# Row sums of 64 MB: the first buffer's two loads, cut by partitions in place of rows

## Chip, cores and metric

The kernel runs on one core of a Trainium2 chip. The metric is the device time of one execution in microseconds (us); the figure given is the median of three executions. The profile is that of one further execution, taken by the hardware profiler.

## What is computed

The input x is a float32 array of 32 x 512 x 1024. The output is the sum over the last axis, one float32 number for each of the 16,384 rows of 1024:

```python
def reference(x: np.ndarray) -> np.ndarray:
    return np.sum(x, axis=-1).astype(np.float32)
```

So 67.11 MB are read from HBM and 65 KB are written. There is one addition for each number read.

## The kernel before

The 16,384 rows are handled in two blocks (BLOCKS = (112, 16)). In a block, each of the 128 partitions owns a run of neighbouring rows: 112 of them in the first block, 16 in the second. Since the rows of a partition lie one behind the other in HBM, a load of 16 rows is, for each partition, one contiguous run of 64 KB in HBM, and goes to 64 KB of that partition in SBUF. Neighbouring partitions start 448 KB apart in HBM.

The first block is read in seven loads of 16 rows (G = 16), 8.39 MB each, into a pool of three buffers called xt. After each load the reduction helper rows_dve (L47) lets VectorE (DVE) sum 16 rows of all partitions in one instruction, from 128x16384 to 128x16 numbers. For the seventh load VectorE sums nine rows and ScalarE (ACT) seven, one activation with an accumulator each (L55). ScalarE then issues the store of the first block's results (L99), as 104 and 24 partitions.

The second block is the end of the kernel. Its 16 rows are loaded in five pieces: 9, 4 and 2 rows into an xt buffer (L105), and the last row in two pieces of 544 and 480 numbers into a tile of its own, tail (L108). VectorE and ScalarE share these pieces, and the store (L128) follows.

What sets the order: all loads are issued by the SP engine, in program order, on one DMA queue (q1 in the profile). The first three buffers are free at the start, so the first four DMAs are issued without a wait; each later load waits on SP until VectorE is done with the buffer that it will fill. The stores of the first block go through ScalarE's queue (q10). A block of code at the end of the file moves SP's first two loads (EARLY = 2) ahead of the start barrier into the entry block of the program.

The first buffer is special. It is filled by two DMAs instead of one, both issued at L89, as the cut points at L87 say:

```python
parts = (0, 1, m) if done + c == 0 else (0, m)
```

That is, for the very first buffer, one row of all 128 partitions (128 runs of 4 KB, 0.5 MB) and then fifteen rows of all 128 partitions (128 runs of 60 KB, 7.5 MB). The reduction of this buffer is one instruction over all sixteen rows, so it waits for both.

Of the kernel before, what the change touches and what calls it, by code (L numbers as in the profile page):

```python
# [1 line left out]

# [4 lines left out]

F32 = mybir.dt.float32
ADD = mybir.AluOpType.add
COPY = mybir.ActivationFunctionType.Copy  # L10
X = mybir.AxisListType.X

BLOCKS = (112, 16)
G = 16
ACT_ROWS = 7
CUT = 544
EARLY = 2


@with_exitstack  # L20
def row_sums(
    ctx: ExitStack,
    tc: tile.TileContext,
    x: bass.AP,
    out: bass.AP,
):
    nc = tc.nc
    P = nc.NUM_PARTITIONS

    x_flat = x.flatten_outer_dims()  # L30
    R, D = x_flat.shape
    C = R // P
    assert R % P == 0 and sum(BLOCKS) == C
    out_flat = out.rearrange("a (b c) -> (a b c)", c=1)

    xpool = ctx.enter_context(tc.tile_pool(name="x", bufs=3))
    rpool = ctx.enter_context(tc.tile_pool(name="res", bufs=1))


    tail = rpool.tile([P, D + 16], F32, name="tail")  # L40
    part = tail[:, CUT + 14 : CUT + 15]
    nc.vector.memset(tail[:, CUT + 15 : CUT + 16], 0.0)  # L42
    seen = rpool.tile([P, 2], F32, name="seen")
    pairs = [rpool.tile([P, D // 2], F32, name=f"pairs{i}") for i in range(3)]

    def rows_dve(xt, res, j, n, c):
        nc.vector.tensor_reduce(  # L47
            out=res[:, c : c + n],
            in_=xt[:, j * D : (j + n) * D].rearrange("p (j d) -> p j d", d=D),
            axis=X,  # L50
            op=ADD,
        )

    def sum_act(v, acc):
        return nc.scalar.activation(out=v, in_=v, func=COPY, accum_out=acc)  # L55

    by_act = []

    def rows_act(xt, res, j, n, c):
        for i in range(n):  # L60
            by_act.append(
                sum_act(xt[:, (j + i) * D : (j + i + 1) * D], res[:, c + i : c + i + 1])
            )

    def pairs_dve(v, a, b, acc, pairs):
        h = (a + b) // 2
        nc.vector.tensor_tensor_reduce(  # L67
            out=pairs[:, 0 : h - a], in0=v[:, a:h], in1=v[:, h:b], scale=1.0, scalar=0.0,
            op0=ADD, op1=ADD, accum_out=acc,
        )  # L70

    def block(r0, n):
        x_b = x_flat[r0 : r0 + P * n].rearrange("(p c) d -> p (c d)", p=P)
        out_b = out_flat[r0 : r0 + P * n].rearrange("(p c) -> p c", p=P)
        return x_b, out_b, rpool.tile([P, n], F32, name=f"res{r0}")

    full = C - G
    done = 0
    for b, n in enumerate(BLOCKS):
        x_b, out_b, res = block(done * P, n)  # L80
        final = b == len(BLOCKS) - 1
        whole = n - G if final else n
        c = 0
        while c < whole:
            m = min(G, whole - c)
            xt = xpool.tile([P, G * D], F32, tag="xt", name="xt")
            parts = (0, 1, m) if done + c == 0 else (0, m)  # L87
            for i, k in zip(parts, parts[1:]):
                nc.sync.dma_start(  # L89
                    out=xt[:, i * D : k * D], in_=x_b[:, (c + i) * D : (c + k) * D]  # L90
                )
            a = ACT_ROWS if done + c + m == full else 0
            rows_dve(xt, res, 0, m - a, c)
            rows_act(xt, res, m - a, a, c + m - a)
            c += m
        if not final:

            for i, k in ((0, 104), (104, P)):
                nc.scalar.dma_start(out=out_b[i:k], in_=res[i:k])  # L99
        done += n  # L100

    xt = xpool.tile([P, G * D], F32, tag="xt", name="xt")
    cuts = [0, 9, 13, 15]
    for i, k in zip(cuts, cuts[1:]):
        nc.sync.dma_start(out=xt[:, i * D : k * D], in_=x_b[:, (c + i) * D : (c + k) * D])  # L105
    last = 15 * D
    for i, k, gap in ((0, CUT, 0), (CUT, D, 16)):
        nc.sync.dma_start(  # L108
            out=tail[:, i + gap : k + gap],
            in_=x_b[:, c * D + last + i : c * D + last + k],  # L110
        )

    by_act.clear()
    for i, k in zip(cuts[:2], cuts[1:3]):
        h = (k - i) // 2
        rows_dve(xt, res, i, h, c + i)
        rows_act(xt, res, i + h, k - i - h, c + i + h)
    pairs_dve(xt, 13 * D, 14 * D, res[:, c + 13 : c + 14], pairs[2])
    rows_act(xt, res, 14, 1, c + 14)
    pairs_dve(tail, 0, CUT, part, pairs[0])  # L120


    nc.vector.tensor_copy(out=seen, in_=tail[:, CUT + 14 : CUT + 16])  # L123
    pairs_dve(tail, CUT + 14, D + 16, res[:, c + 15 : c + 16], pairs[1])


    tc.keep_in_program_order(nc.sync.keepalive_nop([nc.sync.lower_ap(res[:, c + 14 : c + 15])]))
    store = nc.sync.dma_start(out=out_b, in_=res)  # L128
    for i in by_act:
        tc.declare_no_dep(store.ins, i.ins, reason="the wait is in the nop before it")  # L130


def kernel(tc: tile.TileContext, x: bass.AP, out: bass.AP):
    row_sums(tc, x, out)
    tc.close()
    tc.compile()  # L136

    sp = mybir.EngineType.SP  # L140
    fn = tc.nc.m.functions[0]
    entry, body = None, None
    for blk in fn.blocks:
        ops = [i for i in blk.instructions if i.engine == sp]
        if entry is None:
            entry = blk
        elif any(i.opcode == "DMACopy" for i in ops):
            body = blk
            break
    code = list(body.instructions)  # L150
    loads = [i for i in code if i.engine == sp][:EARLY]
    for load in loads:
        assert load.opcode == "DMACopy" and not load.sync_info.on_wait
        code.remove(load)
    body.instructions = code
    code = list(entry.instructions)
    at = next(k for k, i in enumerate(code) if i.engine == sp and i.opcode == "Drain")
    code[at:at] = loads
    entry.instructions = code

# [1 line left out]
_INS = ['x']  # L162
_OUTS = [((32, 512), 'float32')]


# [23 lines left out]
```

## Time and profile before

| what | value |
|---|---|
| median of 3 executions | 162.14 us (162.09 to 162.2) |
| the profiled execution: its own time | 162.21 us |
| the profiled execution: span from first to last instruction | 160.4 us |
| DVE busy | 121.4 us (76%) |
| ACT busy | 17.2 us (11%) |
| HBM read | 67.11 MB, 419 GB/s over the span |
| a reduction of 128x16384 on DVE | 17.22 us |

How to read it: the page gives busy times by engine, the span in 40 slices with the share of the DMA engines and the rate in GB/s in each, the DMA queues with their packets, the chain of work that ended last, and groups of instructions with their mean duration and the idle time ahead of them. A name such as xt<-in_x_dram means that the tile xt is written from the input in HBM. A packet of a queue is one piece of data that one DMA engine moved, or one write of four bytes to a semaphore by which an engine reports that its share of a load is done. There are 16 DMA engines.

### The profile page before, as it was taken

Reading aid. Unit: us, or ns where it says so; the run is one execution under the profiler, and the core shown is the slowest. Engines: PE = TensorE matmul, PEld = TensorE weight load, DVE = VectorE, ACT = ScalarE, POOL = GpSimd, SP = SyncE. Lnnn points to the kernel's source line nnn. Section 1 sums busy time; section 2 is a strip of 40 time slices with the busy share of each in tenths; the row PEclk is TensorE's granted clock in tenths of the full one; section 3 lists DMA queues with packets and bytes.
Section 4 is the critical chain, followed back from the end, with each engine's and each line's share of the span. In section 5 each row is a group of like instructions: output and inputs, shape, how many; then the busy total and the mean of one; then the engine's idle time right before and its main releaser. Section 6 shows DMA issues by size and latency. Waiting matters only on the chain.

```text
span 160.4 us, 122 instructions
## 1 busy us (share of the span) xinstructions
DVE 121.4 (76%) x17; ACT 17.2 (11%) x31; POOL 0.2 (0%) x4
## 2 busy tenths in 40 slices
DVE  0000059997799959999499994999949998698883
ACT  0000000000000000000000000000000000695892
POOL 0000000000000000000000000000000000000000
DMA  9988996996996996996996996997998999998992
GB/s 376 490 368 368 490 523 261 523 523 261 523 523 261 523 523 261 523 523 261 523 507 278 523 490 294 523 474 310 523 425 359 523 392 392 441 395 369 431 393 79
DMA packets 2169, 67.18 MB, mean 419 GB/s; under 512 B 505, under 2 KB 633, under 8 KB 889
## 3 DMA queue, kind: packets, MB, share of 16 engines
q1 hardware_dynamic: 2016, 67.12, 97.4%
q10 hardware_dynamic: 153, 0.06, 0.1%
HBM read 67.11 MB, written 0.07 MB: 419 GB/s over the span
## 4 chain that ended last, share of the span: by engine, by line
DMA 75%; DVE 22%; SPq 0%; issue 0%; DVEq 0%
DMA xt<-in_x_dram 75%; DVE res L47 21%; DVE pairs L67 1%; SPq L105 0%; DVE seen L123 0%; DVE tail L67 0%; DVEq L136 0%; DVE res L67 0%
## 5 line engine op out<-in xcount | busy, mean ns | idle before, releaser
L47 DVE TENSOR_REDUCE res<-xt 128x16 f32<-128x16384 f32 (+3 forms) x9 | 119.8, 13308 | 35.1 <-DMA xt<-in_x_dram 35.1
L55 ACT ACT_TABLE_LOAD x1 | 1.3, 1283 | 137.9 <-DMA xt<-in_x_dram 137.9
L55 ACT ACTIVATE xt<-xt 128x1024 f32<-128x1024 f32 x15 | 15.6, 1043 | 2.5 <-DMA xt<-in_x_dram 2.5
L55 ACT ACTIVATION_READ_ACCUMULATOR xt<-xt 128x1 f32 x15 | 2.8, 186 | 0.0
L42 DVE MEMSET tail<- 128x1 f32 x1 | 0.1, 59 | 1.3 <-PEq L173 1.3
L67 DVE CUSTOM_DVE_ANT_0 pairs<-xt 128x512 f32<-128x512 f32 x1 | 0.7, 692 | 0.3 <-DMA xt<-in_x_dram 0.3
L67 DVE CUSTOM_DVE_ANT_0 pairs<-tail 128x272 f32<-128x272 f32 (+1 forms) x2 | 0.9, 426 | 0.0
L123 DVE COPY seen<-tail 128x2 f32<-128x2 f32 x1 | 0.2, 168 | 0.0
L67 DVE DVE_READ_ACCUMULATOR2_ANT res<- 128x1 f32 x2 | 0.2, 82 | 0.0
L173 POOL MEMSET const-bfloat16-1.0<- 128x1 bf16 x1 | 0.1, 103 | 0.0
L173 POOL MEMSET const-uint8-127<- 128x1 uint8 x1 | 0.1, 102 | 0.0
L173 POOL MEMSET const-float32-1.0<- 128x1 f32 x1 | 0.1, 100 | 0.0
L173 POOL MEMSET const-float32-0.0<- 128x1 f32 x1 | 0.1, 99 | 0.2 <-issue 0.2
L67 DVE DVE_READ_ACCUMULATOR2_ANT tail<- 128x1 f32 x1 | 0.1, 80 | 0.0
## 6 DMA issues: line engine op xcount, KB each, us to landing
xt<-in_x_dram SPq DMA_DIRECT2D x1, 7680.0 KB
xt<-in_x_dram SPq DMA_DIRECT2D x1, 4608.0 KB, 32.6
xt<-in_x_dram SPq DMA_DIRECT2D x1, 2048.0 KB, 37.1
xt<-in_x_dram SPq DMA_DIRECT2D x1, 1024.0 KB, 39.2
xt<-in_x_dram SPq DMA_DIRECT2D x1, 512.0 KB, 3.6
tail<-in_x_dram SPq DMA_DIRECT2D x1, 272.0 KB, 39.3
tail<-in_x_dram SPq DMA_DIRECT2D x1, 240.0 KB, 39.2
xt<-in_x_dram SPq DMA_DIRECT2D x6, 40.8
```

The costliest lines, as they stand in the source:

```text
L42: nc.vector.memset(tail[:, CUT + 15 : CUT + 16], 0.0)
L47: nc.vector.tensor_reduce(out=res[:, c : c + n], in_=xt[:, j * D : (j + n) * D].rearrange("p (j d) -> p j d", d=D), axis=X, op=ADD,)
L55: return nc.scalar.activation(out=v, in_=v, func=COPY, accum_out=acc)
L67: nc.vector.tensor_tensor_reduce(out=pairs[:, 0 : h - a], in0=v[:, a:h], in1=v[:, h:b], scale=1.0, scalar=0.0, op0=ADD, op1=ADD, accum_out ...
L123: nc.vector.tensor_copy(out=seen, in_=tail[:, CUT + 14 : CUT + 16])
L173: nc = _bacc.Bacc("TRN2", target_bir_lowering=False, num_devices=1)
```

## The change

The first buffer is still filled by two DMAs, issued in the same place and order. They are now cut by partitions: first all 16 rows of partitions 0 to 15 (16 runs of 64 KB, 1 MB), then all 16 rows of partitions 16 to 127 (112 runs of 64 KB, 7 MB). The other loads name the same data as before, though they are written in the new form.

```diff
@@ -84,11 +84,10 @@
         while c < whole:
             m = min(G, whole - c)
             xt = xpool.tile([P, G * D], F32, tag="xt", name="xt")
-            parts = (0, 1, m) if done + c == 0 else (0, m)
+
+            parts = (0, 16, P) if done + c == 0 else (0, P)
             for i, k in zip(parts, parts[1:]):
-                nc.sync.dma_start(
-                    out=xt[:, i * D : k * D], in_=x_b[:, (c + i) * D : (c + k) * D]
-                )
+                nc.sync.dma_start(out=xt[i:k, 0 : m * D], in_=x_b[i:k, c * D : (c + m) * D])
             a = ACT_ROWS if done + c + m == full else 0
             rows_dve(xt, res, 0, m - a, c)
             rows_act(xt, res, m - a, a, c + m - a)
```

The lists of instructions of both kernels are the same on every engine but for line numbers (these two loads are issued at L90 instead of L89, and every later line has a number one lower) and the shapes of SP's first two loads: 128x1024 and 128x15360 before, 16x16384 and 112x16384 after.

## The prediction

> **What bounds the kernel now.** I read the slices of the page first, then the timeline of VectorE, then the chain, then stretches cut at the starts of the reductions.
>
> ```profile
> DVE  0000059997799959999499994999949998698883
> ...
> DMA  9988996996996996996996996997998999998992
> GB/s 376 490 368 368 490 523 261 523 523 261 523 523 261 523 523 261 523 523 261 523 507 278 523 490 294 523 474 310 523 425 359 523 392 392 441 395 369 431 393 79
> ```
>
> The DMA row has no gap from the first slice to the last but one. The rates jump between 261 and 523 only because a long packet is booked in one slice; over three slices they are level. VectorE has holes at regular distances. The timeline shows what it waits for there:
>
> ```profile
> 21.84 17.22 DVE L47 TENSOR_REDUCE res<-xt 128x16 f32<-128x16384 f32 x1 [20.46 <-DMA xt<-in_x_dram]
> 41.13 17.22 DVE L47 TENSOR_REDUCE res<-xt 128x16 f32<-128x16384 f32 x1 [2.06 <-DMA xt<-in_x_dram]
> 60.48 17.22 DVE L47 TENSOR_REDUCE res<-xt 128x16 f32<-128x16384 f32 x1 [2.13 <-DMA xt<-in_x_dram]
> 79.82 17.22 DVE L47 TENSOR_REDUCE res<-xt 128x16 f32<-128x16384 f32 x1 [2.12 <-DMA xt<-in_x_dram]
> ```
>
> Columns: start, duration, instruction, idle time ahead and its releaser. A buffer of 8.39 MB arrives every 19.35 us (60.48 - 41.13), its reduction takes 17.22, and the rest is waiting for data. 8.39 MB in 19.35 us are 434 GB/s, 27.1 for each of 16 DMA engines. Each engine carries 8 of the 128 runs of 64 KB, so a run takes 19.35 / 8 = 2.42 us on its engine.
>
> ```profile
> 58.38 40.78 DMA xt<-in_x_dram
> ...
> 117.29 39.21 DMA xt<-in_x_dram
> 156.50 0.02 issue
> 156.52 0.69 DVE pairs L67
> ```
>
> The chain ends with a load and then 1.6 us of short sums. Its reductions (17.23 us pieces) are there because they release the buffers, but a release comes well ahead of need: buffer 1 is free at 21.84 + 17.22 = 39.06, when load 2 has 2 us to go and load 3 is queued whole, some 21 us of DMA work. So the DMA stream never runs dry, and **whatever delays the slowest DMA engine's stream by d at its start delays the end by d**. Nothing later has slack to absorb it.
>
> ```profile
> 0.00:4.00 4.00, 0.06 (x1) 0.00 (x0) 0.20 (x4) 1.00 1.02 377
> 4.00:21.84 17.84, 0.00 (x0) 0.00 (x0) 0.00 (x0) 1.00 1.03 445
> 41.13:60.48 19.35, 17.22 (x1) 0.00 (x0) 0.00 (x0) 1.00 1.00 434
> ```
>
> Columns: stretch and length; DVE, ACT, POOL busy; PE clock; DMA share; GB/s. Even the stretch that holds the change runs near the later rate, so there is little to gain there and much to lose.
>
> [...]
>
> [...]
>
> ```profile
> q1 hardware_dynamic: 2016, 67.12, 97.4%
> q10 hardware_dynamic: 153, 0.06, 0.1%
> ```
>
> ScalarE's queue q10 carries only the stores of 104 and 24 partitions: 128 runs of data and 25 reports, which is 13 (104 / 8) and 12 (24 / 2). Likewise q1: 13 loads of 128 + 16 packets and a store of 144 are 2016. So I expect the new loads on 16 engines each, with 1 and with 7 runs for an engine.
>
> [...]
>
> [...]
>
> [...]
>
> **The change part by part.** The sum starts from the profiled execution: 160.4 us of span and 1.81 outside it make 162.21, 0.07 over the median of 162.14. As the change is a difference within the span, I add it to the median.
>
> *Issue.* Two DMAs before, two after, same place, no wait added. SP's time for them (0.85 us for both in the timeline) stays: 0. Their descriptors are fewer (16 rows, not 128, in the first); the DMA view of the first microseconds has its first bytes at about 1.0 us. I take 0 and keep a small gain for a rival.
>
> *First load, removed.* 0.52 MB in 128 runs, landed 3.6 us after issue; its share of the stream at 434 GB/s is 1.2 us. *First load, added.* 1.05 MB, one run for each engine. [...] Each engine then comes to its next run 9.67 - 2.42 = **7.25 us late**. [...] I take 7.25.
>
> *Second load, added.* 112 runs, 7 for an engine, 16.9 us if no two engines meet. [...] How the runs are dealt out I don't know. I take blocks of seven neighbours: [...] 7 / 4 x 2.42 = **4.2 us**. From below: 0 (later loads fill the holes). From above: [...] 4 x 2.42 = 9.7 us.
>
> *Everything behind.* Six loads of 128 runs[...]: no loss and no recovery, since the engines already run at their full rate. VectorE starts each reduction later by the same amount; it keeps its 2.1 us of idle time for each load, which hides nothing needed. SP's waits for free buffers move along: 21 us of queued work cover them as long as the engines differ by less than that. ScalarE and the end are unchanged: 0.
>
> Sum: 7.25 + 4.2 = 11.45 us. 162.14 + 11.45 = **173.6 us**; from the bounds, 169.4 (7.25 + 0) to 179.1 (7.25 + 9.7).
>
> **The rivals.**
>
> *No change, 162.1.* The DMA engine is the limit[...]. Each engine has 1 + 7 = 8 runs before load 2, as much as before. The same follows if the change doesn't reach the engines as I think: if a partition belonged to an engine whatever the load[...]. For it: 434 GB/s is 16 times one engine's rate[...]. Against it: [...] for the second form the 13 and 12 reports.
>
> *Faster, 161.6.* One mechanism: the cold start. In the view of the first 4 us the first load's data runs from about 1.0 to 3.3 us, 2.3 us for 1.2 us of bytes. So 1.1 us at most are to be won; if it is the short reads that each pay for a cold start, and one long run for each engine pays once, I put the gain at half of that, 0.55 us. [...]
>
> *Much slower, about 213.* If the second load deals neighbouring partitions to different engines in turn, [...] 7 x 7.25 = 51 us. Against it: the engines needn't stay in step[...].
>
> **How the numbers follow.** [...] much slower 5%, no change 11%, faster 12%. A measurement of this kernel can tell about 0.2% (0.3 us) from no change. So faster 0.12, same 0.11, slower 0.77. The likeliest case's own range is 169.4 to 179.1. As it holds only 72%, the range must reach down over the no-change and most of the faster case: 161.5 to 179.1; left out are the much slower case and the tails.
>
> **What would show it.** Right: the first reduction starts near 33 us instead of 21.84, the later ones again 19.35 apart; the rate in the first 10 us falls to about a quarter of 434 GB/s; q1 counts 2016 - 128 = 1888 packets[...]. If the first reduction starts 7 us late and no more, the second load's term is wrong; if it starts over 17 us late, the dealing is. Wrong altogether: the first microseconds at 434 GB/s with 16 partitions being filled, and the first reduction still near 21.8.

## The result and the profile after

| | before | after |
|---|---|---|
| median of 4 executions | 162.12 us (162.04 to 162.2) | 184.4 us (183.82 to 184.55) |
| profiled execution, span | 160.4 us | 182.6 us |
| DVE busy / ACT busy | 121.4 / 17.2 us | 121.4 / 17.2 us |
| first reduction starts | 21.84 us | 44.39 us |

The changed kernel takes 1.137 times as long (95% interval 1.134 to 1.139), 22.3 us more. The forecast was 173.6, in a range of 161.5 to 179.1: the direction was right, the size (11.45 us) was half of what came, and the range was missed.

These are lines of the page of the changed kernel: the 40 slices (each now 182.6 / 40 = 4.6 us long), and the two DMA queues with their packets, megabytes and share.

```profile
DVE  0000000002999599978999599959995999689784
...
DMA  9199799888999988999999988999999989999990
GB/s 230 29 201 230 230 402 215 201 215 330 445 459 459 431 388 373 445 445 459 445 459 459 431 388 373 431 459 445 459 459 459 431 359 402 450 396 421 423 364 14
...
q1 hardware_dynamic: 1888, 67.12, 97.0%
q10 hardware_dynamic: 153, 0.06, 0.1%
```

The DMA row still shows engines that are busy nearly all the time: 97.0% of their time, as before (97.4%). But a busy engine is not one that moves bytes. Of the first nine slices eight show 230 GB/s or less and one 402 (a long packet is booked whole in the slice in which it starts); from the eleventh on the rate is back at its old level. This is how the shortage looks here: a full busy row at half the rate. The 1888 packets are the 2016 of before less 128, so both loads ran on all 16 engines (1 and 7 runs for each), as foretold.

VectorE's timeline in the changed kernel (start, duration, instruction, idle time and its releaser):

```profile
44.39 17.22 DVE L47 TENSOR_REDUCE res<-xt 128x16 f32<-128x16384 f32 x1 [43.01 <-DMA xt<-in_x_dram]
63.67 17.22 DVE L47 TENSOR_REDUCE res<-xt 128x16 f32<-128x16384 f32 x1 [2.06 <-DMA xt<-in_x_dram]
83.02 17.22 DVE L47 TENSOR_REDUCE res<-xt 128x16 f32<-128x16384 f32 x1 [2.13 <-DMA xt<-in_x_dram]
102.36 17.22 DVE L47 TENSOR_REDUCE res<-xt 128x16 f32<-128x16384 f32 x1 [2.12 <-DMA xt<-in_x_dram]
```

All the lost time lies ahead of the first line: 44.39 - 21.84 = 22.55 us. After it the buffers arrive 19.3 us apart, as before, with the same 2.1 us of idle time. Nothing is given back. The short sums at the end of the chain start at 178.71 in place of 156.52, 22.2 us later:

```profile
178.71 0.69 DVE pairs L67
```

Three stretches of the changed kernel: about the first load, most of the second, and the time from the first reduction to the second one (the last column is GB/s):

```profile
1.00:9.00 8.00, 0.06 (x1) 0.00 (x0) 0.00 (x0) 1.00 1.17 147
9.00:39.00 30.00, 0.00 (x0) 0.00 (x0) 0.00 (x0) 1.00 1.03 240
44.39:63.67 19.28, 17.22 (x2) 0.00 (x0) 0.00 (x0) 1.00 0.98 425
```

The kernel before, in the stretch from 9 to 39 us:

```profile
9.00:39.00 30.00, 17.16 (x1) 0.00 (x0) 0.00 (x0) 1.00 1.02 443
```

There are two slow stretches, and the second is the long one. The trace also has each packet. Put in order of their starts and taken 16 at a time (one run of 64 KB for each engine), the packets of the first buffer show how long each run took. Times are in us from the first packet:

```
changed kernel     starts        shortest  median  longest
run 0 (16-load)     0.0 -  0.7     7.64     8.54     9.25
run 1 (112-load)    7.7 -  9.8     5.12     5.47     6.40
run 2              13.7 - 15.0     4.75     4.75     4.90
run 3              18.5 - 19.8     2.98     3.25     4.81
run 4              21.9 - 24.6     3.81     3.89     4.47
run 5              25.8 - 28.4     4.21     4.54     4.84
run 6              30.0 - 33.1     4.71     4.72     4.89
run 7              34.7 - 37.8     4.51     4.53     4.87
```

A line of this table, that is, the 16 runs that the engines carry at the same turn, is called a row of the load below. In a load of 128 partitions such a run takes 2.42 us. Here every run of every engine is slow. In five of the seven rows of the second load even the shortest of 16 runs takes 1.7 to 2.1 times as long. That is not what the prediction had, where the seven rows were to lose 7 / 4 of 2.42 us, 4.2 us in all.

### The profile page after: what moved, and what is told of

Read it like the earlier page. It is cut to its first block, busy times and chain, and to the rows that moved or that the text cites. A ratio compares the mean times of both kernels' runs of the same rounds, so it can differ in the third digit from the quotient of the medians.

```text
span 182.6 us, 122 instructions
## 1 busy us (share of the span) xinstructions
DVE 121.4 (66%) x17; ACT 17.2 (9%) x31; POOL 0.2 (0%) x4
## 3 DMA queue, kind: packets, MB, share of 16 engines
q1 hardware_dynamic: 1888, 67.12, 97.0%
## 4 chain that ended last, share of the span: by engine, by line
DMA 68%; DVE 29%; another core or an unknown queue 1%; SPq 1%; issue 0%; DVEq 0%
DMA xt<-in_x_dram 68%; DVE res L47 28%; DVE pairs L67 1%; SPq L104 0%; SPq L90 0%; DVE seen L122 0%; DVEq L47 0%; DVE tail L67 0%; DVE res L67 0%; DVEq L135 0%
```

## The experiments

All times are medians (of two executions for probe4, probe19 and pstep6, of 22 for nocut, of four for the others), and "over before" is the distance from the median of the kernel before in the same group of runs (162.05 us for the first four, 162.12 for probe11 to probe0 without nocut, 161.97 for nocut, probe4, probe19 and pstep6).

| kernel | us | over before | ratio, 95% interval |
|---|---|---|---|
| eight16 | 216.15 | 54.1 | 1.334 (1.328 to 1.339) |
| step7 | 183.98 | 21.9 | 1.134 (1.131 to 1.138) |
| step8 | 183.44 | 21.4 | 1.131 (1.128 to 1.134) |
| src8 | 217.39 | 55.3 | 1.340 (1.336 to 1.345) |
| probe11 | 167.9 | 5.8 | 1.036 (1.034 to 1.037) |
| probe18 | 174.25 | 12.1 | 1.074 (1.073 to 1.076) |
| probe16 | 172.23 | 10.1 | 1.062 (1.060 to 1.064) |
| probe0 | 181.14 | 19.0 | 1.117 (1.115 to 1.119) |
| nocut | 162.2 | 0.2 | 1.0013 (1.0007 to 1.0020) |
| probe4 | 173.75 | 11.8 | 1.072 (1.070 to 1.075) |
| probe19 | 173.24 | 11.3 | 1.069 (1.067 to 1.071) |
| pstep6 | 172.53 | 10.6 | 1.065 (1.062 to 1.068) |

### How is the second load dealt, and on which side is the limit?

The first four kernels change only how the first buffer is filled. They are built from the changed kernel; the edits of eight16 and src8 are shown against it, those of step7 and step8 against eight16.

*eight16: eight loads of 16 neighbours.*

```diff
-            parts = (0, 16, P) if done + c == 0 else (0, P)
+            cuts = tuple(slice(g, g + 16) for g in range(0, P, 16)) if done + c == 0 else (slice(0, P),)
-            for i, k in zip(parts, parts[1:]):
+            for s in cuts:
-                nc.sync.dma_start(out=xt[i:k, 0 : m * D], in_=x_b[i:k, c * D : (c + m) * D])
+                nc.sync.dma_start(out=xt[s, 0 : m * D], in_=x_b[s, c * D : (c + m) * D])
```

> The first buffer is filled by eight loads of 16 neighbouring partitions each (0-15, 16-31, and so on)[...]. Theory A (the load of 112 partitions deals single partitions to the engines in turn[...]): the runs of each engine are the same as in the changed kernel, so 184 us, within 1.5. Theory B (the 112 partitions are dealt in blocks of seven neighbours[...]): another sequence, [...] eight times 9.67 us in place of 19.35 gives up to 162 + 58 = 220 us, less if an engine's next run overlaps the one before. Theory C ([...] something in HBM or in the count of runs is): unlike both, about 162 plus eight times the 7 us of the first load, 218 us.

Measured 216.15, 54.1 over before. The changed kernel's 184.4 is far off, so theory A (partitions dealt out one at a time) falls. The runs after the first take 9.29 to 9.34 us each. Theories B and C both allow this number; step8 and src8 tell them apart.

*step7: the dealing in blocks of seven, written out as seven loads.*

```diff
-            cuts = tuple(slice(g, g + 16) for g in range(0, P, 16)) if done + c == 0 else (slice(0, P),)
+            cuts = (slice(0, 16),) + tuple(slice(16 + j, P, 7) for j in range(7)) if done + c == 0 else (slice(0, P),)
```

> The load of partitions 0-15 is kept; the other 112 partitions are loaded by seven loads of 16 partitions, each stepping by seven (16, 23, 30, ...)[...]: the dealing in blocks of seven, written out. Theory A: not the order of the changed kernel; [...] the 7.25 us of the first load and 2.4 to 9.7 for the rest: 172 to 179 us. Theory B: the same runs as in the changed kernel, 184 us within 1.5.

Measured 183.98, within 0.5 us of the changed kernel. Its first reduction:

```profile
43.99 17.22 DVE L47 TENSOR_REDUCE res<-xt 128x16 f32<-128x16384 f32 x1 [42.20 <-DMA xt<-in_x_dram]
```

Its runs have the same pattern, row for row: medians 8.56, 5.26, 4.66, 3.11, 4.05, 4.55, 4.65, 4.43 us. So the load of 112 partitions deals blocks of seven neighbours, as the prediction took it (theory B). The dealing was right; the price of it was not.

*step8: eight loads of 16 partitions, eight apart.*

```diff
-            cuts = tuple(slice(g, g + 16) for g in range(0, P, 16)) if done + c == 0 else (slice(0, P),)
+            cuts = tuple(slice(g, P, 8) for g in range(8)) if done + c == 0 else (slice(0, P),)
```

> Eight loads of 16 partitions that step by eight (g, g+8, ..., g+120). [...] Same bytes, same length of run, same 16 engines as eight loads of neighbours. [...] (theories A and B): every run takes twice its 2.42 us, 8 x 4.84 - 19.35 = 19.3 us more than before: 181 us, and no run shorter than 4.7 us in the middle of it. Theory C [...]: the distance between partitions in SBUF makes no difference to it; the same time as eight loads of neighbours.

Measured 183.44, 21.4 over before where theories A and B gave 19.3. Against eight16, with the same bytes, run length, engines and count of loads, a different distance between partitions in SBUF and HBM takes off 33 us. At the median a run takes 5.10 us in six of the seven loads after the first (4.89 in the other), so 16 of them at a time move 16 x 65.5 KB / 5.10 us = 206 GB/s. One stretch in the middle of its filling:

```profile
9.00:39.00 30.00, 0.00 (x0) 0.00 (x0) 0.00 (x0) 1.00 1.02 210
```

210 GB/s are about half of the 434 at which the loads of 128 partitions arrive.

*src8: neighbours in SBUF, eight apart in HBM.*

```diff
-            parts = (0, 16, P) if done + c == 0 else (0, P)
-            for i, k in zip(parts, parts[1:]):
-                nc.sync.dma_start(out=xt[i:k, 0 : m * D], in_=x_b[i:k, c * D : (c + m) * D])
+            if done + c == 0:
+                for g in range(8):
+                    nc.sync.dma_start(
+                        out=xt[16 * g : 16 * g + 16, 0 : m * D],
+                        in_=x_b[g:P:8, c * D : (c + m) * D],
+                    )
+            else:
+                nc.sync.dma_start(out=xt[:, 0 : m * D], in_=x_b[:, c * D : (c + m) * D])
```

> As the eight loads of 16 neighbouring partitions, but each reads its 16 runs of HBM eight partitions apart (the rows of the first 2048 x 7 of the input land in other partitions, so part of the sums stand in another order). [...] (A and B): the same time as the eight loads of neighbours, within 1 us. Theory C with HBM as the cause: the time of the eight loads that step by eight, whose HBM addresses these are.

Measured 217.39, with runs of 9.39 us. That is 1.24 us more than eight16, a little outside the 1 us that was expected at most, and 34 us more than step8. The HBM addresses are those of step8, the time is within 0.6% that of eight16. The limit is on the SBUF side. Theory C falls: its HBM form here, and the form with the count of runs by step8, which has the same count as eight16.

### Is a whole row slow, or a few of its runs?

In the changed kernel each row starts behind another slow one. To look at one set of partitions alone, the kernel before got two additional loads of it, ahead of all else, into the two buffers that are filled later. They fetch data that the later loads overwrite; the sums are those of the kernel before.

```diff
         c = 0
+        if b == 0:
+            for _ in range(2):
+                probe = xpool.tile([P, G * D], F32, tag="xt", name="xt")
+                nc.sync.dma_start(out=probe[11:117:7, :], in_=x_b[11:117:7, 0 : G * D])
         while c < whole:
```

The four kernels of this group have the slices 11:117:7 (probe11, shown above), 18:124:7 (probe18), 16:122:7 (probe16) and 0:16 (probe0). By the dealing that step7 writes out, 16:122:7 is run 1 of the table above and 18:124:7 is run 3; 0:16 is run 0.

> The kernel before, preceded by two additional loads of 16 partitions, 64 KB each, into the two buffers that are not filled first: partitions 11, 18, ..., 116[...]. The cost of the probe is the time over the kernel before. [...] each run takes 2.42 us as in a load of 128 partitions, and the two cost 4.8 us: 167 us. If a load of 16 partitions is slow for another reason (few partitions, runs far apart, one run for each engine), they cost what two loads of partitions 0-15 cost, some 18 us.

Measured 5.8 us for two loads, where 4.8 were expected. The second load's runs take 2.42 to 2.63 us (those of the first 3.23 at the median). So a load of 16 partitions, one run for each engine, far apart, can be as fast as any other: with these partitions it is.

> The same with partitions 18, 25, ..., 123[...]. Theory D[...]: the median run takes well over 2.42 us[...]. Theory E[...]: the median run takes 2.42 us and two of 16 runs 4.8 us; the time is still up to 9.7 us longer, since the two slowed engines set the end.

> The same with partitions 16, 23, ..., 121[...]. Theory D: the median run takes 4.65 us as in the changed kernel, and the two loads cost 9.3 us: 171.4 us. Theory E: four of 16 runs take 4.8 us, the median 2.42 us; the time again up to 9.7 us longer.

> The same with partitions 0 to 15[...]. [...] 9.33 us a run, as in the eight loads of neighbours, 18.7 us for the two: 180.8 us. [...]

The 16 runs of the second probe load, in us:

```
           partitions          fastest 14 runs    slowest 2 runs
probe11    11, 18, ..., 116     2.42 to 2.43       2.43, 2.63
probe18    18, 25, ..., 123     2.42 to 2.48       6.95, 6.99
probe16    16, 23, ..., 121     4.98 to 5.05       5.05, 5.05
probe0     0, 1, ..., 15        9.58 to 9.64       9.64, 9.64
```

The stretch from 6 to 11 us, in which the second probe load gives way to the first real one, in probe11 (the last column is GB/s):

```profile
6.00:11.00 5.00, 0.00 (x0) 0.00 (x0) 0.00 (x0) 1.00 1.15 486
```

The same stretch in probe18:

```profile
6.00:11.00 5.00, 0.00 (x0) 0.00 (x0) 0.00 (x0) 1.00 1.03 290
```

And in probe16:

```profile
6.00:11.00 5.00, 0.00 (x0) 0.00 (x0) 0.00 (x0) 1.00 0.59 123
```

A packet is booked whole where it starts, so 486 and 123 are not rates of the moment; only the order of the three counts, and the table of runs is the better evidence. For the partitions of probe18 theory E holds: 14 runs go at 2.42 to 2.48 us and two are slow. For those of probe16 theory D holds: all 16 take 4.98 to 5.05 us. Neither theory holds for both. The trace doesn't name the engine of a packet, so which partitions the two long runs of probe18 fill is not shown. The size of probe18 was missed: 12.1 us, not up to 9.7. Its two long runs took 6.97 us in the second load, more than twice 2.42. (These runs start at 4.74 and 4.76 us, just as the two slowest runs of the first load end, which fits two engines that are late both times.) By then the other engines were already at the first real load (the 290 GB/s above). Whether that is what makes these two runs so long was not tried.

probe0 prices the first load of the changed kernel by itself: 19.0 / 2 = 9.5 us for each load, 9.5 - 2.42 = 7.1 us more than a load whose runs take 2.42 us.

One thing these probes don't separate: a set of other partitions in SBUF is also a set of other addresses in HBM, and no probe reads the HBM addresses of one set into the partitions of another, as src8 did for the loads of neighbours.

### Two long runs or sixteen: three more sets

The same probe, with the slices 4:110:7, 19:125:7 (run 4 of the table above) and 4:95:6; and one kernel without any cut (nocut, built from the changed kernel).

> The probe of two additional loads, with partitions 4, 11, ..., 109[...]. Theory F[...]: 14 runs of the second load take 2.42 us, two take 4.8 us or more, as with partitions 18 to 123. Theory G[...]: all 16 runs take some 5.0 us, as with partitions 16 to 121.

Measured: 13 of the runs of the second load at 2.42 to 2.59 us, one at 2.65, two at 5.99 and 6.39. As in probe18 only two runs are slow, so theory G falls.

> The probe with partitions 19, 26, ..., 124[...]. Theory F: 14 runs of the second load at 2.42 us, two at 4.8 us or more. [...] if all 16 runs are slow here too, the free engines with partitions 18 to 123 were an exception.

Measured: 13 runs at 2.42 us, one at 2.68, two at 6.32 and 6.49. A third set in which only two runs are slow.

> The probe with partitions 4, 10, ..., 94 (steps of six)[...]. Theory F: all 16 runs of the second load at about 5.0 us, as with partitions 16 to 121[...]. Theory H[...]: part of the runs stay at 2.42 us. [...]

Measured: all 16 runs at 4.96 to 5.11 us, as in probe16. No run stayed at 2.42 us, so theory H falls for this set. The numbers of theory F came in all three sets: of the five sets with long runs in steps of six or seven, three have two long runs and two have sixteen. Why a set belongs to the one kind or the other is not shown; what the author sorted them by beforehand was an assumption. The rows of the 112-load go the same way: run 1, with the partitions of probe16, has a median of 5.47 us, and runs 3 and 4, with those of probe18 and probe19, have 3.25 and 3.89 us (not 2.42. In these rows engines that are late from the row before are still at work, which may be why; this is argued, not tried). Runs 2, 5, 6 and 7 have medians of 4.53 to 4.75 us; their partitions were not tried alone.

*nocut: the first buffer by one load.*

```diff
-EARLY = 2
+EARLY = 1
-            parts = (0, 16, P) if done + c == 0 else (0, P)
+            cuts = (slice(0, P),) if done + c == 0 else (slice(0, P),)
-            for i, k in zip(parts, parts[1:]):
+            for s in cuts:
-                nc.sync.dma_start(out=xt[i:k, 0 : m * D], in_=x_b[i:k, c * D : (c + m) * D])
+                nc.sync.dma_start(out=xt[s, 0 : m * D], in_=x_b[s, c * D : (c + m) * D])
```

> The first buffer is filled by one load of all 128 partitions and 16 rows, without any cut. This tells what the removal of the one-row load is worth by itself in the changed kernel. If the cold start costs each of the short reads of the one-row load, a load of long runs alone starts better: up to 0.55 us faster than before, 161.6 us. If the one-row load starts the stream earlier, this is slower, by up to the 1.1 us that the first 0.5 MB lose now. I expect within 0.3 us of the kernel before: none of the 22 us comes from here.

Measured 162.2 against 161.97, ratio 1.0013 (1.0007 to 1.0020). Taking the one-row load away costs 0.2 us. None of the 22.3 comes from there, and the gain that the "faster" rival hoped for from long runs does not show. No kernel tried is faster than the one before.

## Why the prediction was right and wrong

**The bound and its consequence: right.** The DMA stream sets the time, and a delay at its start goes to the end undiminished: the slowest engine ends the first buffer 42.7 us after its first packet, against 20.4 before. The difference of 22.3 is that of the medians.

**How the loads are dealt: right, in part by luck.** 16 engines each, with one and seven runs, was worked out and came true (1888 packets). That an engine gets a block of seven neighbours was assumed ("How the runs are dealt out I don't know") and turned out right (step7).

**The first load, 7.25 us: right.** In a kernel of its own it costs 7.1 (probe0). That a run would take four times 2.42 us, 9.67, was an assumption that no trace of the kernel before shows; the runs took 9.58 to 9.64 us in probe0 and 9.29 to 9.34 in eight16. There 1.05 MB in 9.33 us are 112 GB/s, about a quarter of 434.

**The second load, 4.2 us: this is the step that failed.** What is left for it is 22.3 - 7.1 = 15.2 us (an estimate, since 7.1 comes from another kernel), beyond its upper end of 9.7. The prediction let 7 / 4 of a row take twice as long, an assumption that no trace of the kernel before shows. As the price of a hindered run twice was right: in run 3 the two longest runs took 4.79 and 4.81 us, twice 2.42. The count was wrong. In five rows of seven all 16 runs are slow, with medians of 4.53 to 5.47 us, and probe16 shows such a row alone: all 16 runs at 4.98 to 5.05 us. Five rows at twice 2.42 us would be 5 x 2.42 = 12.1 us more; the two other rows add 0.8 and 1.5 us by their medians (3.25 and 3.89 less 2.42). That makes 14.4 of the 15.2 (an estimate from these medians).

The range failed with it, since its upper end, 4 x 2.42 = 9.7 us for the second load, was an assumption of the same kind. The dearer rival (about 213) had the wrong dealing; eight16, which is that dealing written out, did take 216.15.

**The order of importance was wrong too.** The prediction put most of the cost in the small load. It is in the large one, which covers 112 of 128 partitions and looks almost like a full load. And the prediction's own sign pointed to the wrong place: it said that a first reduction over 17 us late would show the dealing to be wrong. It was 22.55 us late, and the dealing was right.

**What was ruled out.** No change (the engine is the limit): refuted by step8 against eight16 (5.10 against 9.33 us a run on the same 16 engines). Faster (cold start): refuted by nocut.

**What stays open.** Why one set of 16 partitions slows two of its runs (probe18), another all 16 (probe16), and a third none (probe11) is not shown. Src8 against step8 (217.39 against 183.44 us from the same HBM addresses) puts the limit on the SBUF side; no run here looks inside the path.

## What to carry to other kernels

If a load like this one is to be cut, cut it along the rows of the input, so that each piece keeps all 128 partitions. Here that cut cost nothing against a single load (nocut), and the cut by partitions cost 22.3 us although it left one piece nearly whole. Before cutting by partitions, write down which partitions the engines write at the same turn (the load of 112 partitions gave blocks of seven neighbours to 16 engines, those of 16 partitions one to each) and time such a set alone, as the probes do: of the sets tried one ran at full speed (probe11, 2.42 us a run), three had two long runs (probe18, probe4 and probe19, 6.0 to 7.0 us), two went at half speed (probe16 and pstep6, 5.0 us), and sixteen neighbours at a quarter (probe0, 9.6 us). A DMA row that is full (97.0% busy) while GB/s is half (230 in place of 434) was the sign of this in the profile.

## What the runs showed that was not expected

- Three sets of 16 partitions (probe18, probe4, probe19) have two long runs (the other 14 runs of the second load took 2.42 to 2.68 us). Two sets (probe16, pstep6) have all 16 slow, at 5.0 to 5.1 us. Partitions eight apart (step8) give 5.10 us too.
- Two long runs are not cheap either: the two probe loads of such a set cost 11.3 to 12.1 us, more than those of the sets with 16 long runs (10.1 and 10.6), because the two long runs alone set the end (the last run of the two loads ends 11.75 us after the first packet in probe18, 10.28 in probe16).
- Which partitions a load fills at one time sets its rate: 16 neighbours (eight16) came at 16 x 65.5 KB / 9.33 us = 112 GB/s, 16 partitions eight apart (step8) at 206, and the loads of 128 partitions at 434.
